# A decoder trunk on one core: due times for all work around the product stream, and attention weight tiles split in halves

## The chip, the core and the metric

The kernel runs on one core of a Trainium2 chip. The core has a matrix engine (TensorE, PE in the profile), a vector engine (VectorE, DVE), a scalar engine (ScalarE, ACT), a general engine (GpSimd, POOL) and a queue engine (SyncE, SP), each with its own instruction stream that it works off in order, and sixteen DMA engines. PE multiplies 128x128 blocks that it loads as weights (PEld) with up to 512 columns, into banks of PSUM, an accumulator memory from which DVE and ACT read. Everything else lies in SBUF. The metric is the device time of one execution in microseconds (us), lower is better.

## What is computed

A two-layer decoder trunk for 256 positions of width 2048 in float32. Layer 0 mixes by Mamba-2 SSD heads and latent attention side by side, layer 1 by stick-breaking attention; each is followed by a SwiGLU feed-forward network (FFN) of hidden width 5632. All weights are float32 and are read once.

```python
for layer in range(DEPTH):                       # DEPTH = 2
    h = rms_norm(x, mix_norm[layer])
    if layer % 2 == 0:
        mix = ssd_mla_mixer(h, w_in[e], ..., w_out_even[e], cos, sin)
    else:
        mix = stick_breaking_mixer(h, w_qkv[o], w_out_odd[o])
    x = x + mix
    f = rms_norm(x, ffn_norm[layer])
    x = x + (silu(f @ w_gate[layer]) * (f @ w_up[layer])) @ w_down[layer]
return rms_norm(x, final_norm)
```

## The kernel before

**Split products.** A float32 matrix is taken apart into a rounded part and a remainder, and each product is made of three: hi by hi, hi by lo, lo by hi. A weight tile is 4 k-tiles of 128 rows by 512 columns, 1 MB, loaded by one DMA on SP's queue. `split` (line 247) makes `wh` (a cast on ACT, line 249) and `wl` (a subtraction on DVE, line 250), each 128x2048. Activations are split in the same way after PE has transposed them (`transpose_split`, PE line 259).

**Projections.** `project` (line 333) runs over the k-tiles of a column block for two row tiles (6 matmuls of 512 columns for each k-tile, lines 340 to 342), with weights from `load_split` (line 300). After an output projection `add_residual` (line 390) adds the two accumulators to the residual `xres` (DVE line 395, one operation for each row tile), and the next layer's transposes read `xres`.

**The FFN.** `ffn` (line 550) goes over the hidden width in five blocks of 2, 2, 2, 2 and 3 column pairs; after each block come four down projections. `pair` (line 467) computes a 512-column block of gate and of up together. Over the first 8 of 16 k-tiles it uses a Strassen-like scheme of seven products, each 12 matmuls (`product`, lines 493, 494 and 498); over the last 8 the four tiles are multiplied plainly ("classical", lines 526 to 528, 24 matmuls each). The scheme needs the weight tiles b11, b22, b21 and the sums t1 = b11 + b12, t2 = t1 + b22, t3 = b12 + b22 and t4 = t2 + b21 (`wadd`, DVE line 464, 128x2048 each), all split. PE uses them in the order b11, b22, t1, b21, t2, t4, t3, then the four classical tiles. At the end of a pair `left` (h-, DVE line 558, then SiLU on ACT) and `right` (for row tile 1 H*, line 566; for row tile 0 h+, line 564, and then H*, line 566) turn the accumulators into `h`, which PE transposes in the middle of the next pair's first products.

**Where tiles lie.** A "region" of SBUF, `xp`, changes its use: in the attention layers ("acts") it holds activations, in an FFN ("sums") the sums and some weight tiles. A new region's tiles wait for the old region's last readers at the places that they overlay. `wh` and `wl` have two buffers each in the pool `weights`, and in an FFN every third tile lies in the region (`whtile`, `wltile`, lines 109 and 112). Loaded tiles `w` have three, and in an FFN one more in the region.

**What sets the order.** PE's order is that of the program text. On the other engines a scheduler orders by priority (a lower number comes first) as dependences allow. Weight work (loads, splits, sums) takes numbers from a counter, `wprio`, that starts at 100000 and rises with each piece, so it goes in the order of the text. Work marked URGENT has 50000. Everything else, the residual adds among it, has 10000000: it goes after weight work that is ready. `tick` (line 81) counts units of the product stream, `now`; background tasks (transposes, attention chains) are generators that `tick` moves on.

Of the kernel before, what the change touches and what calls it, by code (L numbers as in the profile page):

```python
# [27 lines left out]
class Trunk:  # L28
# [6 lines left out]
    def __init__(self, ctx, tc, ins, out):  # L35
        self.tc, self.nc, self.i, self.out = tc, tc.nc, ins, out
        ec = ctx.enter_context
        self.cp = ec(tc.tile_pool(name="const", bufs=1))
        self.wp = ec(tc.tile_pool(name="weights", bufs=4))
        self.ap = ec(tc.tile_pool(name="acts", bufs=42))  # L40
        self.sp = ec(tc.tile_pool(name="small", bufs=2))
        ps = bass.MemoryType.PSUM
        self.pacc = ec(tc.tile_pool(name="pacc", bufs=1, space=ps))
        self.ptr = ec(tc.tile_pool(name="ptr", bufs=4, space=ps))
        self.dp = ec(tc.tile_pool(name="scratch", bufs=1, space=bass.MemoryType.DRAM))
        self.shared, self.shared_kind = None, None
        self.region("acts")
        ctx.callback(self.region, None)
        self.banks = ["acc0", "acc1", "acc2", "acc3"]
        self.n, self.wn = 0, {}  # L50
        self.now, self.tasks = 0, []
        self.wprio = 100000
        tc.cur_priority = 10000000

    @contextmanager
    def priority(self, at):

        keep, self.tc.cur_priority = self.tc.cur_priority, at
        yield
        self.tc.cur_priority = keep  # L60


    def spawn(self, gen):
# [16 lines left out]

    def tick(self):
        self.now += 1
        ready = [t for t in self.tasks if t["wake"] <= self.now]
        for t in ready[:2]:
            if not t["done"]:
                self.advance(t)

    def region(self, kind):

        if self.shared is not None:  # L90
            self.shared.__exit__(None, None, None)
        self.shared, self.shared_kind = None, kind
        if kind:
            bufs = 20 if kind == "acts" else 2
            self.shared = self.tc.tile_pool(name=f"shared_{kind}", bufs=bufs, reuse_waits="tile")
            self.xp = self.shared.__enter__()

    def s2x(self, shape, dt=F32):

        return self.xp.tile([P, *shape], dt, name=self.nm("s2x"), tag="s2x", bufs=20)  # L100

    def wtile(self, tag="w", dt=F32, bufs=4, own=3):

        n = self.wn[tag] = self.wn.get(tag, 0) + 1
        if self.shared_kind == "sums" and n % bufs == 0:
            return self.xp.tile([P, 4, 512], dt, name=self.nm(tag), tag=tag, bufs=1)
        return self.wp.tile([P, 4, 512], dt, name=self.nm(tag), tag=tag, bufs=own)

    def whtile(self):
        return self.wtile("wh", F32R, 3, 2)  # L110

    def wltile(self):
        return self.wtile("wl", F32R, 3, 2)

    def wsum(self):
        return self.xp.tile([P, 4, 512], F32, name=self.nm("wsum"), tag="wsum", bufs=2)
# [25 lines left out]
    def constants(self):  # L142
# [4 lines left out]
        with self.priority(0):  # L147
            nc.sync.dma_start(rows_m, i["mix_norm"].rearrange("l (k p) -> (l k) p", p=P))
        for j in range(4):
            with self.priority(self.wprio + 1000 * j - 500):  # L150
                nc.sync.dma_start(self.xres[:, :, j * 512:(j + 1) * 512],
                                  i["x"][0, :, j * 512:(j + 1) * 512].rearrange("(t p) d -> p t d", p=P))
        with self.priority(self.wprio + 3500):
            self.small_loads(rows_a, rows_b)
        with self.priority(self.wprio + 6500):
# [144 lines left out]
    def load_split(self, view, nk, n):  # L300

        nc = self.nc
        for k0 in range(0, nk, 4):
            k1 = min(nk, k0 + 4)
            res = []
            with self.priority(self.wprio):
                self.wprio += 1000
                w = self.wtile()
                for dst, src in view(w, k0, k1):
                    nc.sync.dma_start(dst, src)  # L310
                order = ExitStack()
                for ins in self.first if self.wprio <= 105000 else ():
                    order.enter_context(self.tc.issue_after(ins))
                wh, wl = self.whtile(), self.wltile()
                step = 1 if self.wprio < 102000 else 2 if self.wprio < 106000 else k1 - k0
                for c in range(0, k1 - k0, step):
                    d = c + step
                    self.split(wh[:, c:d, :n], wl[:, c:d, :n], w[:, c:d, :n])
                order.close()
                for k in range(k0, k1):  # L320
                    res.append((wh[:, k - k0, :n], wl[:, k - k0, :n]))
            yield from res

    @staticmethod
# [65 lines left out]
    def add_residual(self, ps, j, scale=None):  # L390
        nc, x = self.nc, self.xres
        for t in range(2):
            xs = x[:, t, j * 512:(j + 1) * 512]
            if scale is None:
                nc.vector.tensor_tensor(xs, ps[t], xs, op=ALU.add)
            else:
                nc.vector.scalar_tensor_tensor(xs, ps[t], scale[:, t:t + 1], xs, op0=ALU.mult, op1=ALU.add)


    URGENT = 50000  # L400
# [42 lines left out]
            res.append((hi, lo))  # L443
        return res

    def wload(self, view, k0):
        w = self.wtile()
        with self.priority(self.wprio):
            self.wprio += 100
            for dst, src in view(w, k0, k0 + 4):  # L450
                self.nc.sync.dma_start(dst, src)
        return w

    def wsplit(self, w):
        wh, wl = self.whtile(), self.wltile()
        with self.priority(self.wprio):
            self.wprio += 100
            self.split(wh, wl, w)
        return wh, wl

    def wadd(self, o, p, q):
        with self.priority(self.wprio):
            self.wprio += 100
            self.nc.vector.tensor_tensor(o, p, q, op=ALU.add)
        return o

    def pair(self, st, xT, va, vb, left, right):
# [1 line left out]

        nc = self.nc  # L470
        mm = nc.tensor.matmul
        b11, b12 = self.wload(va, 0), self.wload(vb, 0)
        b22, b21 = self.wload(vb, 4), self.wload(va, 4)
        cl = [(self.wload(va, 8), self.wload(vb, 8)), (self.wload(va, 12), self.wload(vb, 12))]
        t1 = self.wadd(self.wsum(), b11, b12)
        w11 = self.wsplit(b11)
        t2 = self.wadd(self.wsum(), t1, b22)
        t3 = self.wadd(b12, b12, b22)
        w22 = self.wsplit(b22)
        wt1 = self.wsplit(t1)  # L480
# [645 lines left out]
```

## Time and profile before

| | before |
|---|---|
| device time, median of 3 runs | 2513.11 us (2512.77 to 2513.15) |
| the profiled execution's own time | 2512.09 us |
| its span in the trace | 2510.4 us |
| granted TensorE clock, mean | 0.991 |
| PE busy | 2454.1 us, 98% of the span |
| DVE busy | 1714.3 us, 68% |
| ACT busy | 1298.1 us, 52% |
| instructions | 27612 |

A row of a group or timeline has the line of the kernel, the engine, the operation, what it writes and reads, and busy time with the mean in ns, or start and duration in us. In brackets stands the idle time before an instruction and what ended it. A row of a window has the busy time and count of PE, PEld, DVE, ACT and POOL, the granted clock, the DMA share and GB/s.

### The profile page before, as it was taken

How to read it: one execution, taken by the hardware profiler on the slowest of the kernel's cores; microseconds unless marked ns; L12 is line 12 of the kernel's file. 1: busy time of each engine (PE TensorE's matmuls, PEld its weight loads, DVE VectorE, ACT ScalarE, POOL GpSimd, SP SyncE). 2: the span in 40 equal slices, each digit the busy share in tenths (PEclk: the TensorE clock that was granted, in tenths of full speed). 3: DMA queues.
4: the chain of work that ended last, by engine and by line, in shares of the span. 5: the costliest groups of instructions: out<-in, count | busy, mean ns of one | idle time of the engine just before them, and what ended most of it. 6: DMA issues, size and time to landing. Idle time of an engine off the chain costs nothing.

```text
span 2510.4 us, 27612 instructions
## 1 busy us (share of the span) xinstructions
PE 2454.1 (98%) x11176; PEld 2008.4 (80%) x11176; DVE 1714.3 (68%) x1476; ACT 1298.1 (52%) x1266; POOL 130.9 (5%) x164
## 2 busy tenths in 40 slices
PE   8999999999899999999999999999899999999998
PEld 7788877788688888888878787778688888888876
DVE  5775455456778778787965444445787878787874
ACT  6655555434554545454544545554554545454553
POOL 1231121000000000000000000000000000000001
PEclk9999999999899999999999999999999999999999
DMA  7654553355555556565554454445555656565653
GB/s 234 194 176 159 178 157 111 126 193 185 182 197 199 194 196 206 184 203 185 204 190 143 166 172 160 151 155 173 181 200 184 217 172 215 170 231 168 235 188 114
DMA packets 257824, 454.78 MB, mean 181 GB/s; under 512 B 20716, under 2 KB 45424, under 8 KB 257696
## 3 DMA queue, kind: packets, MB, share of 16 engines
q1 hardware_dynamic: 255168, 446.48, 53.1%
q0 software_dynamic: 1952, 5.48, 0.6%
q8 instruction: 88, 1.44, 0.2%
q10 hardware_dynamic: 576, 1.05, 0.1%
q14 instruction: 40, 0.33, 0.0%
HBM read 450.85 MB, written 2.13 MB: 180 GB/s over the span
## 4 chain that ended last, share of the span: by engine, by line
PE 56%; issue 39%; ACT 2%; DVE 1%; POOL 0%; DMA 0%; SPq 0%; POOLq 0%; ACTq 0%; DVEq 0%
PE acc L341 11%; PE acc L340 11%; PE acc L342 11%; PE acc L527 3%; PE acc L526 3%; PE acc L528 3%; PE acc L493 3%; PE acc L494 3%; PE acc L498 3%; PE tr L259 1%; ACT wh L249 1%; DVE wl L250 1%; PE at L1049 1%; PE at L978 1%; PE at L1048 0%
## 5 line engine op out<-in xcount | busy, mean ns | idle before, releaser
L250 DVE TENSOR_TENSOR wl<-w,wh 128x2048 fp32r<-128x2048 f32 (+2 forms) x431 | 966.3, 2250 | 578.3 <-ACT wh L249 569.5
L249 ACT CAST wh<-w 128x2048 fp32r<-128x2048 f32 (+2 forms) x431 | 807.3, 1875 | 732.5 <-PE acc L342 414.8
L340 PE MATMUL acc<-wh,s 128*128 128x512 f32 (+1 forms) x1728 | 692.2, 401 | 3.3 <-ACT wh L249 3.3
L341 PE MATMUL acc<-wl,s 128*128 128x512 f32 (+1 forms) x1728 | 673.6, 390 | 7.0 <-DVE wl L250 6.9
L342 PE MATMUL acc<-wh,s 128*128 128x512 f32 (+1 forms) x1728 | 674.2, 390 | 0.0
L341 PEld LDWEIGHTS acc<-wl,s 128*128 128x128 f32 x1728 | 326.2, 189 | 74.4 <-DVE wl L250 10.3
L342 PEld LDWEIGHTS acc<-wh,s 128*128 128x128 f32 x1728 | 325.3, 188 | 70.2
L340 PEld LDWEIGHTS acc<-wh,s 128*128 128x128 f32 x1728 | 325.9, 189 | 67.6 <-ACT wh L249 4.1
L528 PE MATMUL acc<-wl,s 128*128 128x512 f32 x704 | 275.3, 391 | 0.0
L527 PE MATMUL acc<-wh,s 128*128 128x512 f32 x704 | 275.2, 391 | 0.0
L526 PE MATMUL acc<-wh,s 128*128 128x512 f32 x704 | 275.2, 391 | 0.0
L493 PE MATMUL acc<-wh,s 128*128 128x512 f32 x616 | 246.4, 400 | 0.0
L494 PE MATMUL acc<-wh,s 128*128 128x512 f32 x616 | 242.4, 393 | 0.0
L249 ACT CAST wh<-wsum 128x2048 fp32r<-128x2048 f32 x66 | 125.9, 1910 | 84.6 <-PE acc L527 35.7
L498 PE MATMUL acc<-wl,s 128*128 128x512 f32 x616 | 166.1, 391 | 0.0
L250 DVE TENSOR_TENSOR wl<-wsum,wh 128x2048 fp32r<-128x2048 f32 x66 | 150.6, 2285 | 13.8 <-ACT wh L249 13.8
L527 PEld LDWEIGHTS acc<-wh,s 128*128 128x128 f32 x704 | 132.2, 188 | 29.1
L526 PEld LDWEIGHTS acc<-wh,s 128*128 128x128 f32 x704 | 132.2, 188 | 29.0
L528 PEld LDWEIGHTS acc<-wl,s 128*128 128x128 f32 x704 | 132.1, 188 | 29.0
L493 PEld LDWEIGHTS acc<-wh,s 128*128 128x128 f32 x616 | 116.9, 190 | 25.6
L494 PEld LDWEIGHTS acc<-wh,s 128*128 128x128 f32 x616 | 117.0, 190 | 24.3
L498 PEld LDWEIGHTS acc<-wl,s 128*128 128x128 f32 x616 | 115.8, 188 | 25.7
(246 smaller groups left out, 2063.3 us busy)
## 6 DMA issues: line engine op xcount, KB each, us to landing
w<-in_w_gate_dram SPq DMA_DIRECT2D x88, 1024.0 KB, 5.1
w<-in_w_up_dram SPq DMA_DIRECT2D x88, 1024.0 KB, 5.1
w<-in_w_down_dram SPq DMA_DIRECT2D x88, 1024.0 KB, 5.0
w<-in_w_qkv_dram SPq DMA_DIRECT2D x48, 1024.0 KB, 5.0
w<-in_w_in_dram SPq DMA_DIRECT2D x47, 1024.0 KB, 5.2
w<-in_w_out_even_dram SPq DMA_DIRECT2D x32, 1024.0 KB, 4.9
w<-in_w_out_odd_dram SPq DMA_DIRECT2D x16, 1024.0 KB, 5.0
w<-in_w_ukv_dram SPq DMA_DIRECT2D x32, 256.0 KB, 4.1
```

The lines of the kernel that those rows point to most:

```text
L249: nc.scalar.copy(hi, src)
L250: nc.vector.tensor_tensor(lo, src, hi.bitcast(F32), op=ALU.subtract)
L259: self.nc.tensor.transpose(pt[:, k, t * P:(t + 1) * P], src(t, 2 * k2 + k), self.ident)
L340: nc.tensor.matmul(ps[t], hi[:, ts], wh, start=k == 0, stop=False)
L341: nc.tensor.matmul(ps[t], hi[:, ts], wl, start=False, stop=False)
L342: nc.tensor.matmul(ps[t], lo[:, ts], wh, start=False, stop=k == nk - 1)
L493: mm(ps, hi[:, k], wh[:, k], start=start and k == 0, stop=False, skip_group_check=True)
L494: mm(ps, lo[:, k], wh[:, k], start=False, stop=False, skip_group_check=True)
L498: mm(ps, hi[:, k], wl[:, k], start=False, stop=k == 3, skip_group_check=True)
L526: mm(ps, hi, wh, start=False, stop=False, skip_group_check=True)
L527: mm(ps, lo, wh, start=False, stop=False, skip_group_check=True)
L528: mm(ps, hi, wl, start=False, stop=stop, skip_group_check=True)
```

## The change

The counter goes. A piece of weight work is now due at a unit of the product stream: `due(units)` is 100000 + 250 x (now + units). `tick` sets the number of all other work to `due(4)`, so it stands among the weight work instead of behind all of it. The residual adds become URGENT. `wh` and `wl` move into the region altogether (`part`): in attention layers as halves of 2 k-tiles with 4 buffers each, in an FFN as whole tiles with 3 buffers each, all in the region. `load_split` splits a tile in two halves in attention layers. `pair` loads b11, b22, b12, b21 in this order, and splits and sums are written in the order in which PE needs them, with due offsets. Nothing on PE changes. The instructions that the halves add are 155 on ACT and 155 on DVE.

```diff
-        self.n, self.wn = 0, {}
+        self.n = self.wn = 0
-        self.wprio = 100000
+        self.base = 100000
         tc.cur_priority = 10000000
+    def due(self, units):
+        return self.base + 250 * (self.now + units)
     def priority(self, at):
...
     def tick(self):
         self.now += 1
+        self.tc.cur_priority = self.due(self.SLACK)
         ready = [t for t in self.tasks if t["wake"] <= self.now]
         for t in ready[:2]:
             if not t["done"]:
...
     def region(self, kind):
         if self.shared is not None:
             self.shared.__exit__(None, None, None)
         self.shared, self.shared_kind = None, kind
         if kind:
-            bufs = 20 if kind == "acts" else 2
-            self.shared = self.tc.tile_pool(name=f"shared_{kind}", bufs=bufs, reuse_waits="tile")
+            self.shared = self.tc.tile_pool(name=f"shared_{kind}", bufs=2, reuse_waits="tile")
             self.xp = self.shared.__enter__()
     def s2x(self, shape, dt=F32):
         return self.xp.tile([P, *shape], dt, name=self.nm("s2x"), tag="s2x", bufs=20)
-    def wtile(self, tag="w", dt=F32, bufs=4, own=3):
-        n = self.wn[tag] = self.wn.get(tag, 0) + 1
-        if self.shared_kind == "sums" and n % bufs == 0:
-            return self.xp.tile([P, 4, 512], dt, name=self.nm(tag), tag=tag, bufs=1)
-        return self.wp.tile([P, 4, 512], dt, name=self.nm(tag), tag=tag, bufs=own)
-    def whtile(self):
-        return self.wtile("wh", F32R, 3, 2)
-    def wltile(self):
-        return self.wtile("wl", F32R, 3, 2)
+    def wtile(self):
+        self.wn += 1
+        pool, bufs = (self.xp, 1) if self.shared_kind == "sums" and self.wn % 4 == 0 else (self.wp, 3)
+        return pool.tile([P, 4, 512], F32, name=self.nm("w"), tag="w", bufs=bufs)
+    def part(self, tag):
+        nk, bufs = (2, 4) if self.shared_kind == "acts" else (4, 3)
+        return self.xp.tile([P, nk, 512], F32R, name=self.nm(tag), tag=tag, bufs=bufs)
     def wsum(self):
         return self.xp.tile([P, 4, 512], F32, name=self.nm("wsum"), tag="wsum", bufs=2)
...
         for k0 in range(0, nk, 4):
             k1 = min(nk, k0 + 4)
             res = []
-            with self.priority(self.wprio):
-                self.wprio += 1000
+            with self.priority(self.due(0)):
                 w = self.wtile()
                 for dst, src in view(w, k0, k1):
                     nc.sync.dma_start(dst, src)
                 order = ExitStack()
-                for ins in self.first if self.wprio <= 105000 else ():
+                for ins in self.first if self.now < 16 else ():
                     order.enter_context(self.tc.issue_after(ins))
-                wh, wl = self.whtile(), self.wltile()
-                step = 1 if self.wprio < 102000 else 2 if self.wprio < 106000 else k1 - k0
-                for c in range(0, k1 - k0, step):
-                    d = c + step
-                    self.split(wh[:, c:d, :n], wl[:, c:d, :n], w[:, c:d, :n])
+                np = 2 if self.shared_kind == "acts" else 4
+                for a in range(k0, k1, np):
+                    b = min(k1, a + np)
+                    wh, wl = self.part("wh"), self.part("wl")
+                    step = 1 if self.now < 4 else np
+                    for c in range(0, b - a, step):
+                        d = min(c + step, b - a)
+                        self.split(wh[:, c:d, :n], wl[:, c:d, :n], w[:, a - k0 + c:a - k0 + d, :n])
+                    for k in range(a, b):
+                        res.append((wh[:, k - a, :n], wl[:, k - a, :n]))
                 order.close()
-                for k in range(k0, k1):
-                    res.append((wh[:, k - k0, :n], wl[:, k - k0, :n]))
             yield from res
     @staticmethod
...
         nc, x = self.nc, self.xres
         for t in range(2):
             xs = x[:, t, j * 512:(j + 1) * 512]
-            if scale is None:
-                nc.vector.tensor_tensor(xs, ps[t], xs, op=ALU.add)
-            else:
-                nc.vector.scalar_tensor_tensor(xs, ps[t], scale[:, t:t + 1], xs, op0=ALU.mult, op1=ALU.add)
+            with self.priority(self.URGENT):
+                if scale is None:
+                    nc.vector.tensor_tensor(xs, ps[t], xs, op=ALU.add)
+                else:
+                    nc.vector.scalar_tensor_tensor(xs, ps[t], scale[:, t:t + 1], xs, op0=ALU.mult, op1=ALU.add)
     URGENT = 50000
...
             res.append((hi, lo))
         return res
-    def wload(self, view, k0):
+    def wload(self, view, k0, at):
         w = self.wtile()
-        with self.priority(self.wprio):
-            self.wprio += 100
+        with self.priority(self.due(at)):
             for dst, src in view(w, k0, k0 + 4):
                 self.nc.sync.dma_start(dst, src)
         return w
-    def wsplit(self, w):
-        wh, wl = self.whtile(), self.wltile()
-        with self.priority(self.wprio):
-            self.wprio += 100
+    def wsplit(self, w, at):
+        wh, wl = self.part("wh"), self.part("wl")
+        with self.priority(self.due(at)):
             self.split(wh, wl, w)
         return wh, wl
-    def wadd(self, o, p, q):
-        with self.priority(self.wprio):
-            self.wprio += 100
+    def wadd(self, o, p, q, at):
+        with self.priority(self.due(at)):
             self.nc.vector.tensor_tensor(o, p, q, op=ALU.add)
         return o
...
         nc = self.nc
         mm = nc.tensor.matmul
-        b11, b12 = self.wload(va, 0), self.wload(vb, 0)
-        b22, b21 = self.wload(vb, 4), self.wload(va, 4)
-        cl = [(self.wload(va, 8), self.wload(vb, 8)), (self.wload(va, 12), self.wload(vb, 12))]
-        t1 = self.wadd(self.wsum(), b11, b12)
-        w11 = self.wsplit(b11)
-        t2 = self.wadd(self.wsum(), t1, b22)
-        t3 = self.wadd(b12, b12, b22)
-        w22 = self.wsplit(b22)
-        wt1 = self.wsplit(t1)
-        t4 = self.wadd(self.wsum(), t2, b21)
-        w21 = self.wsplit(b21)
-        wt2, wt4, wt3 = self.wsplit(t2), self.wsplit(t4), self.wsplit(t3)
+        b11, b22, b12, b21 = (self.wload(*a) for a in ((va, 0, 0), (vb, 4, 2), (vb, 0, 4), (va, 4, 6)))
+        cl = [(self.wload(va, 8, 14), self.wload(vb, 8, 18)), (self.wload(va, 12, 22), self.wload(vb, 12, 26))]
+        w11, w22 = self.wsplit(b11, 0), self.wsplit(b22, 2)
+        t1 = self.wadd(self.wsum(), b11, b12, 4)
+        wt1 = self.wsplit(t1, 4)
+        w21 = self.wsplit(b21, 6)
+        t2 = self.wadd(self.wsum(), t1, b22, 8)
+        wt2 = self.wsplit(t2, 8)
+        wt4 = self.wsplit(self.wadd(self.wsum(), t2, b21, 10), 10)
+        wt3 = self.wsplit(self.wadd(b12, b12, b22, 12), 12)
         self.join(st["xT"][0][0])
         self.join(st["xT"][1][0])
         z, p3, p2, p4 = self.banks
...
         for half in range(2):
             k0, last = 8 + 4 * half, half == 1
             for side in range(2):
-                wh, wl = self.wsplit(cl[half][side])
+                wh, wl = self.wsplit(cl[half][side], 0)
                 if not last:
                     for k in range(4):
                         for t, ps in enumerate((p2, p4) if side == 0 else (p3, z)):
```

The instructions move in these places, all on DVE. In the rows `wl` is a split's remainder, `wsum` or a `w` written from two tiles a sum of weights, `xres` a residual add, and `s` from `acc` a step of `h`.

The start of the first FFN, around the end of the attention layer's last output projection (the two `xres` rows). Before:

```order
L250 TENSOR_TENSOR wl_5152<-w_5133,wh_5151 128x2048
L395 TENSOR_TENSOR xres<-acc_4941,xres 128x512
L464 TENSOR_TENSOR wsum_5149<-w_5133,w_5135 128x2048
L250 TENSOR_TENSOR wl_5159<-w_5137,wh_5158 128x2048
L464 TENSOR_TENSOR wsum_5155<-wsum_5149,w_5137 128x2048
L464 TENSOR_TENSOR w_5135<-w_5135,w_5137 128x2048
L250 TENSOR_TENSOR wl_5163<-wsum_5149,wh_5162 128x2048
L395 TENSOR_TENSOR xres<-acc_4942,xres 128x512
```

Now:

```order
L255 TENSOR_TENSOR wl_5436<-w_5429,wh_5435 128x1024
L403 TENSOR_TENSOR xres<-acc_5299,xres 128x512
L403 TENSOR_TENSOR xres<-acc_5300,xres 128x512
L469 TENSOR_TENSOR wsum_5531<-w_5507,w_5511 128x2048
L255 TENSOR_TENSOR wl_5524<-w_5507,wh_5523 128x2048
L255 TENSOR_TENSOR wl_5528<-w_5509,wh_5527 128x2048
L255 TENSOR_TENSOR wl_5534<-wsum_5531,wh_5533 128x2048
```

Both residual adds moved ahead of the first pair's work; the split of b11, which stood ahead of them (`wl_5152`), moved behind them.

The change from the first to the second pair of the second block. Before, from the sum t2 on:

```order
L464 TENSOR_TENSOR wsum_7079<-wsum_7073,w_7061 128x2048
L558 TENSOR_TENSOR s_1193_6856<-acc_6842,s_1193_6856 128x512
L250 TENSOR_TENSOR wl_7076<-w_7057,wh_7075 128x2048
L558 TENSOR_TENSOR s_1196_6935<-acc_6843,s_1196_6935 128x512
L464 TENSOR_TENSOR w_7059<-w_7059,w_7061 128x2048
L566 SCALAR_TENSOR_TENSOR s_1196_6935<-acc_6840,rstd_5125,s_1196_6935 128x512
L250 TENSOR_TENSOR wl_7083<-w_7061,wh_7082 128x2048
L564 TENSOR_TENSOR s_1195_6909<-acc_6841,s_1195_6909 128x512
L566 SCALAR_TENSOR_TENSOR s_1193_6856<-s_1195_6909,rstd_5125,s_1193_6856 128x512
```

Now:

```order
L255 TENSOR_TENSOR wl_6620<-w_6603,wh_6619 128x2048
L561 TENSOR_TENSOR s_1259_6402<-acc_6388,s_1259_6402 128x512
L561 TENSOR_TENSOR s_1262_6481<-acc_6389,s_1262_6481 128x512
L469 TENSOR_TENSOR wsum_6637<-wsum_6627,w_6605 128x2048
L569 SCALAR_TENSOR_TENSOR s_1262_6481<-acc_6386,rstd_5499,s_1262_6481 128x512
L255 TENSOR_TENSOR wl_6624<-w_6605,wh_6623 128x2048
L567 TENSOR_TENSOR s_1261_6455<-acc_6387,s_1261_6455 128x512
L469 TENSOR_TENSOR w_6607<-w_6607,w_6605 128x2048
L569 SCALAR_TENSOR_TENSOR s_1259_6402<-s_1261_6455,rstd_5499,s_1259_6402 128x512
```

The sums t2 and t3 each come one step of `h` later; t3 (`w_6607`) now stands between h+ (L567) and the last H* (L569). The sum t4 moved as well, from ahead of the split of b21 to behind that of t2.

The end of the first layer's FFN and the start of the stick-breaking layer. Before:

```order
L250 TENSOR_TENSOR wl_9729<-w_9726,wh_9728 128x2048
L270 SCALAR_TENSOR_TENSOR s_1614_9664<-tr_9658,vm,s_1613_9663 128x256 x2
L270 SCALAR_TENSOR_TENSOR s_1617_9681<-tr_9675,vm,s_1616_9680 128x256 x2
L250 TENSOR_TENSOR wl_9767<-w_9764,wh_9766 128x2048
L250 TENSOR_TENSOR wl_9823<-w_9820,wh_9822 128x2048
L395 TENSOR_TENSOR xres<-acc_9638,xres 128x512
L395 TENSOR_TENSOR xres<-acc_9639,xres 128x512
```

Now:

```order
L255 TENSOR_TENSOR wl_10103<-w_10100,wh_10102 128x2048
L275 SCALAR_TENSOR_TENSOR s_1806_10038<-tr_10032,vm,s_1805_10037 128x256 x2
L275 SCALAR_TENSOR_TENSOR s_1809_10055<-tr_10049,vm,s_1808_10054 128x256 x2
L403 TENSOR_TENSOR xres<-acc_10012,xres 128x512
L403 TENSOR_TENSOR xres<-acc_10013,xres 128x512
L255 TENSOR_TENSOR wl_10141<-w_10138,wh_10140 128x1024
L255 TENSOR_TENSOR wl_10145<-w_10138,wh_10144 128x1024
```

The attention layer's first two splits (`wl_9767`, `wl_9823`) stood ahead of the last residual adds; the first half (`wl_10141`) now stands behind them.

More of the change, by code (lines that the diff above doesn't have):

```diff
@@ L60, in priority @@
         self.tc.cur_priority = keep
+    SLACK = 4
     def spawn(self, gen):
@@ L149, in constants @@
         for j in range(4):
-            with self.priority(self.wprio + 1000 * j - 500):
+            with self.priority(self.base + 1000 * j - 500):
                 nc.sync.dma_start(self.xres[:, :, j * 512:(j + 1) * 512],
                                   i["x"][0, :, j * 512:(j + 1) * 512].rearrange("(t p) d -> p t d", p=P))
-        with self.priority(self.wprio + 3500):
+        with self.priority(self.base + 3500):
             self.small_loads(rows_a, rows_b)
-        with self.priority(self.wprio + 6500):
+        with self.priority(self.base + 6500):
             self.wdt = []
```

## The prediction, made before the changed kernel ran

> **What bounds the kernel now.** I read the page first (busy shares), then the waits of PE, then windows of 40 us, then the timelines of DVE, ACT and PE around each gap.
>
> ```profile
> PE 2454.1 (98%) x11176; PEld 2008.4 (80%) x11176; DVE 1714.3 (68%) x1476; ACT 1298.1 (52%) x1266; POOL 130.9 (5%) x164
> PE tr L259 <- DVE xres L395: 22.7, 2, 11.4
> PE acc L341 <- DVE wl L250: 8.7, 6, 1.8
> PE acc L340 <- ACT wh L249: 4.3, 5, 1.1
> PE tr L259 <- DVE s L566: 4.3, 2, 2.2
> 600.00:640.00 40.00, 40.00 (x178) 32.48 (x177) 26.40 (x25) 19.91 (x22) 0.00 (x0) 1.00 0.56 187
> 640.00:680.00 40.00, 28.65 (x120) 23.20 (x119) 33.90 (x28) 23.37 (x23) 0.00 (x0) 0.83 0.50 174
> 1240.00:1280.00 40.00, 37.81 (x163) 30.67 (x162) 35.81 (x23) 23.57 (x18) 0.00 (x0) 0.96 0.54 182
> 1760.00:1800.00 40.00, 28.54 (x123) 23.02 (x122) 27.99 (x26) 19.25 (x25) 0.00 (x0) 0.87 0.46 157
> 2360.00:2400.00 40.00, 37.89 (x170) 30.93 (x169) 36.45 (x24) 22.28 (x17) 0.00 (x0) 1.00 0.59 207
> L250 DVE TENSOR_TENSOR wl<-w,wh 128x2048 fp32r<-128x2048 f32 x415 | 949.3, 2295 | 573.1 <-ACT wh L249 564.3 <-DMA w<-in_w_ukv_dram 5.1 <-PE acc L528 3.4
> L249 ACT CAST wh<-w 128x2048 fp32r<-128x2048 f32 x415 | 792.7, 1910 | 725.0 <-PE acc L342 409.9 <-PE acc L527 119.3 <-DVE xres L395 66.0
> ```
>
> PE is the bound: 2454.1 us busy. An undisturbed window holds 178 matmuls in 40 us, about 0.227 us each with the odd record missing, so a Strassen product of 12 takes 2.73. The change keeps PE's order and work, so all it can move is the idle time: two waits of 11.4 us at the FFN starts (22.7), two of 2.2 at pair changes (4.3), and 13.0 on `wl` and `wh`, mostly in the stick-breaking layer. Not all of that can be had: the rest of PE's idle time is the start and the end.
>
> **FFN starts (gain).** DVE, then PE:
>
> ```profile
> 640.43 0.69 DVE L395 TENSOR_TENSOR xres<-acc,xres 128x512 f32<-128x512 f32 x1 [0.65 <-PE acc L342]
> 641.04 2.28 DVE L464 TENSOR_TENSOR wsum<-w,w 128x2048 f32<-128x2048 f32 x1
> 649.85 2.28 DVE L250 TENSOR_TENSOR wl<-wsum,wh 128x2048 fp32r<-128x2048 f32 x1
> 652.05 0.68 DVE L395 TENSOR_TENSOR xres<-acc,xres 128x512 f32<-128x512 f32 x1
> 640.71 0.40 PE L342 MATMUL acc<-wh,s2x 128*128 128x512 f32 x1
> 652.79 1.76 PE L259 MATMUL tr<-ident,xres 128*128 128x128 f32 x7 [11.28 <-DVE xres L395]
> 675.00 0.39 PE L526 MATMUL acc<-wh,s 128*128 128x512 f32 x1
> ```
>
> The second residual add stands behind five operations of 2.28 us that start every 2.20 (641.04 to 652.05). From the projection's end E (640.71 + 0.23 = 640.94) to the first classical tile at 675.00 there are 34.1 us; unstalled it would be eight transposes (1.76) and 7 x 2.73 = 20.9. The loss is 13.2; the second FFN start, whose window is alike, gives 12.5 by the same walk. After the change both residual adds come first, so the transposes end at E+2.65. But no split and no sum of the first pair is ahead of the residuals any more (the `wh`, `wl` and `wsum` tiles now lie in the region that the projection still uses). DVE pays them in line: `wsum` to E+3.05, `wl11` 5.2, `wl22` 7.4, `wl` of t1 9.6; ACT casts 1.91 each and copies z between them. My walk has the third product over at 13.9, the splits of t2, t4, t3 at 20.8, 25.5, 27.9, and the classical tile effectively at E+29.9: a loss of 9.0. Gain 4.2 + 3.5 = 7.7. Bounds: all 25.7 (the first pair is split early after all) to a loss of 3 (one more 2.28 in line at some point).
>
> **Pair changes (loss).** In each FFN block the next pair begins on PE while DVE finishes `h` of the last: h+ (L564), then H* (L566), then PE's transposes. C is the end of the pair's last matmul. First a change without a stall (953.21 is C - 0.39), then the one with:
>
> ```profile
> 951.86 2.28 DVE L250 TENSOR_TENSOR wl<-w,wh 128x2048 fp32r<-128x2048 f32 x1
> 954.06 0.68 DVE L564 TENSOR_TENSOR s<-acc,s 128x512 f32<-128x512 f32 x1
> 954.77 0.75 DVE L566 SCALAR_TENSOR_TENSOR s<-s,rstd,s 128x512 f32<-128x512 f32 x1
> 953.21 0.39 PE L528 MATMUL acc<-wl,s 128*128 128x512 f32 x1
> 956.23 0.60 PE L259 MATMUL tr<-ident,s 128*128 128x128 f32 x4
> 1252.80 0.68 DVE L564 TENSOR_TENSOR s<-acc,s 128x512 f32<-128x512 f32 x1
> 1254.14 2.29 DVE L250 TENSOR_TENSOR wl<-wsum,wh 128x2048 fp32r<-128x2048 f32 x1 [0.66 <-ACT wh L249]
> 1256.35 0.74 DVE L566 SCALAR_TENSOR_TENSOR s<-s,rstd,s 128x512 f32<-128x512 f32 x1
> 1251.94 0.39 PE L528 MATMUL acc<-wl,s 128*128 128x512 f32 x1
> 1257.24 0.63 PE L259 MATMUL tr<-ident,s 128*128 128x128 f32 x4 [2.19 <-DVE s L566]
> 1257.62 0.48 PE L493 MATMUL acc<-wh,s 128*128 128x512 f32 x1
> ```
>
> With h+ and H* side by side H* ends at C+1.92 and the transposes, due at C+2.63, wait for nothing: 0.7 us of slack. At 1252 one split stands between them, and PE waits 2.19. In the order of before that is so at two of the twelve changes, the two with the 4.3 us of waits. In the new order each of the twelve has an operation of 2.28 us there: in blocks 2 to 4, and the first change of block 5, the sum t3; in block 1 and the second change of block 5 a split of t1. So h+ runs C+0.46 to 1.14, the sum holds DVE until C+3.3, H* ends at C+4.05 and the transposes start at 4.2, a stall of 1.6. Nothing can hide that: h+ needs the accumulator that C closes, DVE runs in order, and PE has one product (2.73 us) to do meanwhile. The split type stalls 2.35 as measured (start to start).
>
> Behind it DVE is a big operation later than before, and the sum t4 now stands after `wl` of t2: 14.5 us after C, its cast (1.91) ends at 16.5, `wl` of t4 at 18.7, where PE, 1.6 late, wants the cast at 15.9. The last classical split ends at 23.1 against 22.8 wanted. That is 1.4 to 1.6 more: about 3.2 per change. Block 1, by the same walk from 2.35, comes to 3.9. The second change of block 5 had 2.35 already, and gains 1.5 in cost. Per FFN 3.9 + 4 x 3.2 + 1.5 = 18.2, for two 36.4. Lower bound, the first stall alone: 2 x (2.35 + 4 x 1.6) = 17.5. Upper bound: two operations of 2.28 late at each of the ten new places, 2 x 5 x 4.6 = 46, and 1.5 more at the two old ones, 49. I take 36.4, as both parts follow from an order that is fixed. After the stall at 1257 the matmuls start 0.32 to 0.43 apart for some 3 us, and the window's granted clock is 0.96; the other stall (2360 to 2400) left it at 1.00. I take 0.3 a change, +3.5 in all; bounds 0 and 12 x 1.8 = 21.6.
>
> The Trainium skill ("TensorE: Matmul & The Clock Gate", Part 1) says that the array falls to half rate after an idle window of about 3.4 us and is back after as long a busy one. By that rule the new stalls, all under 3.4, would cost no clock, and the sum would be 3.5 lower; the trace agrees at 2392 and not at 1257.
>
> **Stick-breaking layer (gain).**
>
> ```profile
> 1440.00:1480.00 40.00, 37.65 (x171) 31.28 (x172) 21.04 (x20) 19.91 (x23) 0.00 (x0) 0.96 0.48 158
> L250 DVE TENSOR_TENSOR wl<-w,wh 128x1024 fp32r<-128x1024 f32 x12 | 14.4, 1220 | 5.3 <-ACT wh L249 5.2
> L249 ACT CAST wh<-w 128x1024 fp32r<-128x1024 f32 x12 | 12.3, 1051 | 7.5 <-PE acc L342 5.0 <-DMA w<-in_w_ukv_dram 1.5 <-DMA w<-in_w_in_dram 0.8
> 1513.60 0.53 ACT L691 ACTIVATE s<-s 128x384 f32<-128x384 f32 x1 [2.24 <-POOL s L689]
> 1518.48 1.90 ACT L249 CAST wh<-w 128x2048 fp32r<-128x2048 f32 x1
> 1520.43 0.49 PE L340 MATMUL acc<-wh,s 128*128 128x512 f32 x1 [1.01 <-ACT wh L249]
> 1522.76 0.50 PE L341 MATMUL acc<-wl,s 128*128 128x512 f32 x1 [1.83 <-DVE wl L250]
> ```
>
> At each of four V projections the cast stands behind the chain of POOL's selects and ACT's exponentials; PE waits 1.01 and 1.83, 3.3 start to start. A half takes 1.05 and 1.22 instead of 1.91 and 2.295, 0.9 and 1.1 less, but the chain stays ahead of the cast and the second half's cast follows it: about 1.9 of the 3.3 stay, gain 4 x 1.4 = 5.6, bounds 0 and 13. In the even layer, whose waits are the rest of the 13.0 and gaps of 0.4 us, halves take about 3.5; bounds -1 and 6. At the second layer's start the two residual adds (which wait for the projection's end) now stand ahead of the first attention split: 0.69 + 0.6 and half a split on DVE put `wl` 2.0 us behind that end, and PE 1.8; bounds 0 and 4. The 155 extra instructions on ACT and DVE are these halves: 155 x (2 x 1.22 - 2.295) = 22 us more on DVE and 30 on ACT. The window shows both half idle beside PE there (21.04 and 19.91 of 40), so I cost them at nothing; without that cover they would be those 22 to 30.
>
> **Sum:** 36.4 + 3.5 - 7.7 - 5.6 - 3.5 + 1.8 = +24.9 on the profiled 2512.1: 2537.0. The runs' median (2513.1) lies 1.0 above the profiled execution, so 2538.
>
> **Rivals.** *The later part of each pair change is hidden* (0.19): only the first stall counts, because t4's cast and split finish in time. For it: the chain is late by only 0.3 to 1 us at each step; against: t4's sum, cast and split follow one another, 2.2 + 1.9 + 2.2, with nothing to overlap them. With clock 2 and 15.0 of gains: 2513 + 17.5 + 2 - 15 = about 2518, or 2513 to 2523. *The gains win* (0.24; not slower): the first pair of each FFN is ready at E+2.7, because the casts there start as soon as the projection's next-to-last matmul is done and residuals no longer wait. FFN starts give 24, stick-breaking 11, the even layer 5, against 17.5: 2490 to 2507. It decides if the splits of t1 and t2 keep up with PE, that is if DVE needs under 2.73 per product; five splits and sums for the first three products speak against it. *The new order does nothing on balance* (0.07), gains and stalls half as large as I have them: 2508 to 2518. *Cold after every stall* (0.07): 1.8 us at all twelve instead of the mean of 0.3: 2538 + 12 x 1.5 = 2556.
>
> **How the numbers follow.** My forecast, 2538, has 0.43; its own range is 2525 to 2551. Two runs of this kernel can be told apart from 0.2% on, 5 us. Faster 0.24; within 0.2% the 0.07 and 0.05 of the first rival, 0.12; slower the rest, 0.64. The range reaches down into the faster case and up to the forecast's dearer end: 2499 to 2553.
>
> **What would show it.** Waits of PE: the transposes on DVE's H* twelve times at 1.6 to 2.4 us instead of two; no 11-us wait on the residual, but waits on `wl` and `wh` in the first pair after it; DVE's timeline with a 2.28-us operation between h+ and H*; halves as 128x1024 groups. Wrong if those transposes start without a wait, or if the first pair's splits run before the residuals.

## The result and the profile after

| | before | after |
|---|---|---|
| device time, median | 2513.13 us (2512.77 to 2519.43, 4 runs) | 2549.49 us (2547.41 to 2552.76, 4 runs) |
| ratio | 1 | 1.014, 95% interval 1.0121 to 1.0159 |
| the profiled execution's span | 2510.4 us | 2547.3 us |
| granted TensorE clock, mean | 0.991 | 0.996 |
| PE busy | 2454.1 us | 2492.2 us |

The change made the kernel 36 us slower; the forecast was 25 slower. Most of it does not come from where the forecast had it. First the changed kernel's page (busy time) and its waits of PE (us in total, times, longest):

```profile
PE 2492.2 (98%) x11176; PEld 2002.5 (79%) x11176; DVE 1737.2 (68%) x1631; ACT 1318.9 (52%) x1421; POOL 129.3 (5%) x164
PE tr L264 <- DVE s L569: 17.7, 12, 2.2
PE acc L501 <- DVE wl L255: 8.7, 18, 1.6
PE acc L496 <- ACT wh L254: 5.4, 10, 1.8
PE acc L348 <- DVE wl L255: 2.1, 2, 1.7
PE tr L264 <- DVE xres L403: 0.7, 2, 0.4
PE acc L347 <- ACT wh L254: 0.6, 1, 0.6
```

The waits changed much as forecast: twelve on H* (L569) instead of two, the two of 11.4 us on the residual down to 0.4 each, new ones on splits inside the Strassen products (L496, L501), and the 13.0 us on `wh` and `wl` of the projections down to 2.7. But in sum the waits that PE names are about as long as before (45 us against 47). What grew by 38 us is PE's **busy** time, with the same 11176 instructions and a higher granted clock. One group shows it: a third of the classical matmuls, first of the kernel before, then of the changed one.

```profile
L527 PE MATMUL acc<-wh,s 128*128 128x512 f32 x704 | 275.2, 391 | 0.0
```

```profile
L529 PE MATMUL acc<-wh,s 128*128 128x512 f32 x704 | 277.9, 395 | 0.0
```

The mean of one went from 391 to 395 ns. PE is pipelined, so what counts is the time from one start to the next: over the 512-column matmuls on split tiles whose successor starts within 0.3 us, its mean is 229.2 ns before and 232.5 after. The program has 9816 matmuls on split tiles, of which some 9300 have such a successor: 9816 x 3.3 ns is about 33 us of the 36.9 between the spans. The rest, some 4 us, is what losses and gains of the order leave on balance.

**FFN start**, changed kernel; PE, then DVE:

```profile
642.64 0.39 PE L349 MATMUL acc<-wh,s2x 128*128 128x512 f32 x1
643.81 0.98 PE L264 MATMUL tr<-ident,xres 128*128 128x128 f32 x7 [0.35 <-DVE xres L403]
672.09 0.40 PE L529 MATMUL acc<-wh,s 128*128 128x512 f32 x1
642.39 1.37 DVE L403 TENSOR_TENSOR xres<-acc,xres 128x512 f32<-128x512 f32 x2 [7.89 <-PE acc L349]
643.67 2.28 DVE L469 TENSOR_TENSOR wsum<-w,w 128x2048 f32<-128x2048 f32 x1
645.87 4.48 DVE L255 TENSOR_TENSOR wl<-w,wh 128x2048 fp32r<-128x2048 f32 x2
```

Both residual adds run at once and the transposes follow, but DVE idles 7.89 us ahead of them, and the first pair's sum and splits come after. From the projection's last matmul to the first classical one there are 29.45 us instead of 34.29 (second FFN 29.45 instead of 33.66).

**Pair change**, changed kernel; DVE, then PE:

```profile
963.95 0.68 DVE L567 TENSOR_TENSOR s<-acc,s 128x512 f32<-128x512 f32 x1
964.55 2.28 DVE L469 TENSOR_TENSOR w<-w,w 128x2048 f32<-128x2048 f32 x1
966.75 0.74 DVE L569 SCALAR_TENSOR_TENSOR s<-s,rstd,s 128x512 f32<-128x512 f32 x1
963.31 0.39 PE L531 MATMUL acc<-wl,s 128*128 128x512 f32 x1
963.54 0.40 PE L496 MATMUL acc<-wh,s 128*128 128x512 f32 x1
967.63 0.63 PE L264 MATMUL tr<-ident,s 128*128 128x128 f32 x4 [1.13 <-DVE s L569]
```

The sum t3 stands between h+ (L567) and H* (L569), and PE waits 1.13 us. The two starts 963.31 and 963.54 are 0.23 apart in both kernels to two digits; the 5 ns do not show in a timeline row, only in a mean.

**Stick-breaking layer.** PE's sum over four windows of 80 us (1400 to 1720), before and then changed:

```profile
sum 320.00, PE 308.85 PEld 255.13 DVE 151.91 ACT 165.99 POOL 18.91; mean PE 77.21 PEld 63.78 DVE 37.98 ACT 41.50 POOL 4.73
```

```profile
sum 320.00, PE 320.00 PEld 263.80 DVE 164.69 ACT 181.88 POOL 9.68; mean PE 80.00 PEld 65.95 DVE 41.17 ACT 45.47 POOL 2.42
```

The 11.15 us of idle PE are gone altogether.

### The profile page after: what moved, and what is told of

Read it like the earlier page. It is cut to its first block, busy times and chain, and to the rows that moved or that the text cites. A ratio compares the mean times of both kernels' runs of the same rounds, so it can differ in the third digit from the quotient of the medians.

```text
span 2547.3 us, 28045 instructions
## 1 busy us (share of the span) xinstructions
PE 2492.2 (98%) x11176; PEld 2002.5 (79%) x11176; DVE 1737.2 (68%) x1631; ACT 1318.9 (52%) x1421; POOL 129.3 (5%) x164
## 4 chain that ended last, share of the span: by engine, by line
PE 84%; DVE 9%; ACT 3%; issue 2%; DMA 1%; POOL 0%; SPq 0%; ACTq 0%; DVEq 0%; POOLq 0%
PE acc L347 18%; PE acc L349 18%; PE acc L348 18%; PE acc L531 5%; PE acc L530 5%; PE acc L529 5%; DVE wl L255 5%; PE acc L501 3%; PE acc L496 3%; PE acc L497 3%; ACT wh L254 2%; DVE wsum L469 1%; PE tr L264 1%; DVE w L469 1%; PE at L1052 1%
## 5 line engine op out<-in xcount | busy, mean ns | idle before, releaser
L255 DVE TENSOR_TENSOR wl<-w,wh 128x1024 fp32r<-128x1024 f32 (+2 forms) x586 | 999.9, 1712 | 582.3 <-ACT wh L254 580.9
L254 ACT CAST wh<-w 128x1024 fp32r<-128x1024 f32 (+2 forms) x586 | 831.6, 1425 | 836.0 <-PE acc L349 469.8
L348 PE MATMUL acc<-wl,s 128*128 128x512 f32 (+1 forms) x1728 | 679.0, 393 | 2.2 <-DVE wl L255 2.1
L348 PEld LDWEIGHTS acc<-wl,s 128*128 128x128 f32 x1728 | 325.7, 189 | 73.5 <-DVE wl L255 3.6
L531 PE MATMUL acc<-wl,s 128*128 128x512 f32 x704 | 279.4, 397 | 2.6 <-DVE wl L255 2.1
L530 PE MATMUL acc<-wh,s 128*128 128x512 f32 x704 | 278.0, 395 | 0.0
L529 PE MATMUL acc<-wh,s 128*128 128x512 f32 x704 | 277.9, 395 | 0.0
L496 PE MATMUL acc<-wh,s 128*128 128x512 f32 x616 | 250.0, 406 | 7.3 <-ACT wh L254 5.4
L497 PE MATMUL acc<-wh,s 128*128 128x512 f32 x616 | 244.5, 397 | 0.0
L501 PE MATMUL acc<-wl,s 128*128 128x512 f32 x616 | 172.0, 401 | 8.7 <-DVE wl L255 8.7
L501 PEld LDWEIGHTS acc<-wl,s 128*128 128x128 f32 x616 | 115.9, 190 | 43.6 <-DVE wl L255 16.9
L496 PEld LDWEIGHTS acc<-wh,s 128*128 128x128 f32 x616 | 116.8, 190 | 41.2 <-ACT wh L254 11.2
L497 PEld LDWEIGHTS acc<-wh,s 128*128 128x128 f32 x616 | 116.9, 190 | 24.9
```

The source lines that it names most:

```text
L254: nc.scalar.copy(hi, src)
L255: nc.vector.tensor_tensor(lo, src, hi.bitcast(F32), op=ALU.subtract)
L348: nc.tensor.matmul(ps[t], hi[:, ts], wl, start=False, stop=False)
L496: mm(ps, hi[:, k], wh[:, k], start=start and k == 0, stop=False, skip_group_check=True)
L497: mm(ps, lo[:, k], wh[:, k], start=False, stop=False, skip_group_check=True)
L501: mm(ps, hi[:, k], wl[:, k], start=False, stop=k == 3, skip_group_check=True)
```

## Why a matmul takes longer: four kernels with padding

The matmuls sort by one property. (Counts of matmuls here and below hold to a few, their means to 0.1 ns.) Each reads a moving tile (`wh` or `wl`, 512 columns of 4 bytes) and loads a stationary tile (activations). In the kernel before, `wh` and `wl` lie mostly in the pool `weights`, in the changed one all in the region. Their start addresses in a partition, as the built programs have them, differ by whole multiples of 512 bytes for 6581 of the matmuls before (mean 227.7 ns) and by 128 or 384 for 2737 (232.5 to 232.8). After, by a multiple of 512 for 734 (227.4 ns) and by 128 for 8516 (233.0). **Theory A** is that this difference sets the pace; the rivals are the place in SBUF or the waits for it (B), and stalls (C). Unused bytes between two pools move one pool against the other and leave every instruction where it is:

```diff
 # after_p384, before_p384: 96 floats; after_p128: 32 floats, ahead of the region
+        self.sp.tile([P, 96], F32, name="pad", tag="pad", bufs=1)
 # before_a128: 32 floats, ahead of the activations, behind the weights
+        self.ap.tile([P, 32], F32, name="pad", tag="pad", bufs=1)
```

> 384 unused bytes per partition between the pool of activations and the region; no instruction changes its place. Theory A (a 512-column matmul costs about 5 ns more when the start addresses of its moving tile, wh or wl, and its stationary tile differ by something other than a multiple of 512 bytes; here all 9815 of them then differ by a multiple): the mean pitch in the feed-forward layers falls from 233 to 228 ns, and the time by about 8516 x 5.3 = 45 us, from 2549 to 2502 to 2508 us. Rival B (tiles in the region are slow because the region lies high in SBUF, or because its buffers are waited for): the region only moves up by 384 bytes, so the time stays at 2545 to 2553. Rival C (the added time is stalls by the new order): the same, 2545 to 2553.

> The kernel before with the same 384 bytes. Theory A: its 2011 matmuls at 128 and 725 at 384 bytes of difference lose about 5 ns each, 14 us: 2497 to 2502 us. Rivals B and C: 2511 to 2515.

> The kernel before with 128 unused bytes ahead of the activations, so that the weight tiles and the activations, which differed by a multiple of 512 for 7007 matmuls, now differ by 384 more; the order stays. Theory A: 6581 measured matmuls cost 5.3 ns more, +35 us, 2543 to 2552; 768 matmuls come to a difference of 256 and tell that one. Rivals B and C: 2511 to 2515.

> The changed kernel with 128 bytes of padding: 9047 matmuls have a difference of 256 instead of 128. Theory A with a period of 512 bytes: still 232 to 233 ns, 2543 to 2553 us. Theory A with a period of 256 bytes: 227 to 228 ns, 2502 to 2508 us. Rivals B and C: 2545 to 2553.

| kernel | us, median | ratio to before, 95% | matmuls and mean ns from start to start, by the difference modulo 512 |
|---|---|---|---|
| before_p384 | 2499.06 | 0.9942 (0.9926 to 0.9959) | 0: 9305 at 227.3 |
| before_a128 | 2545.90 | 1.0136 (1.0119 to 1.0153) | 128: 2015 at 233.2; 256: 732 at 227.0; 384: 6570 at 232.9 |
| after_p384 | 2526.27 | 1.0054 (1.0039 to 1.0069) | 0: 9231 at 227.5 |
| after_p128 | 2520.99 | 1.0033 (1.0020 to 1.0045) | 0: 734 at 227.2; 256: 8497 at 227.5 |

The same kind of group row in three of them, before_p384, before_a128 and after_p384 in this order:

```profile
L527 PE MATMUL acc<-wh,s 128*128 128x512 f32 x704 | 273.9, 389 | 0.0
```

```profile
L527 PE MATMUL acc<-wh,s 128*128 128x512 f32 x704 | 278.0, 395 | 0.0
```

```profile
L529 PE MATMUL acc<-wh,s 128*128 128x512 f32 x704 | 274.0, 389 | 0.0
```

Theory A stands and B falls: 128 bytes make the kernel before 33 us slower, 384 bytes in another place make it 14 faster, with the same order of instructions. The 391 ns of the kernel before are a mixture: two thirds of the FFN's tiles at 389 (own buffers), one third at 394 (region). A difference of 256 is as good as none, so the period is 256 bytes. The changed kernel, though, came to 2526 (after_p384) and 2521 (after_p128) and not to 2502 to 2508: its matmuls are at 227.5 ns, but its waits on H* grew from 17.7 us to this (after_p384):

```profile
PE tr L264 <- DVE s L569: 27.6, 12, 3.4
```

The twelve pair changes take 14 us more than in the changed kernel; 10 of it are these waits, and behind several of them matmuls stand 0.43 us apart. A faster PE gives DVE less time, and the new order's stalls, partly covered by the slow matmuls, come out: over the 180 matmuls of a pair, 5.5 ns are 1 us, and the wait of the eight common changes grew on average by that (1.1 to 2.2 us). This is worked out, not tested by itself. At equal pace the order costs 2526.27 - 2499.06 = 27 us, or 22 by after_p128, whose eight runs reach from 2514 to 2527.

**How fine the difference is.** Two more kernels have 8 and 16 floats in the place of before_a128's 32.

> The kernel before with 32 unused bytes ahead of the activations: 7007 matmuls then have weight tile and activation 224 bytes apart by a period of 256 (the region's stay at 128). If any difference costs 5 ns: +33 to 37 us, 2544 to 2550, as with 128 bytes. If only bit 7 of the two start addresses has to agree (they end in hexadecimal 40 and 60 here): 227 ns as before, 2511 to 2516 us. If the cost grows with the difference: between, 2518 to 2535.

> The same with 64 bytes: 192 apart by a period of 256, and the starts end in hexadecimal 40 and 80. Any difference, or bit 7: 2544 to 2550 us. If the cost grows with the difference: between that of 32 and of 128 bytes.

They took 2549.76 us (ratio 1.0145, 1.0131 to 1.0159) and 2544.82 (1.0126, 1.0113 to 1.0140). The 6575 matmuls 224 apart (modulo 256) have 233.2 ns, the 6573 at 192 the same; 725 at 96 have 233.4, 732 at 64 have 229.2. So neither one address bit nor the size of the difference alone decides; the differences of 96, 128, 192 and 224 all cost 5 to 6 ns. Only the 64 is milder, and only one group of matmuls in one kernel had it.

## Which part of the order costs, and which gains

All five kernels here have the 384 bytes, so that pace plays no part.

**The pair changes.** after_p384_h puts three things on DVE behind the last H* of the pair before:

```diff
+    def behind(self):
+        return ExitStack() if self.lasth is None else self.tc.issue_after(self.lasth.ins)
...
-        wt1 = self.wsplit(t1, 4)
+        with self.behind():
+            wt1 = self.wsplit(t1, 4)
...
-        wt3 = self.wsplit(self.wadd(b12, b12, b22, 12), 12)
+        with self.behind():
+            wt3 = self.wsplit(self.wadd(b12, b12, b22, 12), 12)
...
-            nc.vector.scalar_tensor_tensor(h[t], c, rstd[:, t:t + 1], h[t], op0=ALU.mult, op1=ALU.mult)
+            self.lasth = nc.vector.scalar_tensor_tensor(h[t], c, rstd[:, t:t + 1], h[t], op0=ALU.mult, op1=ALU.mult)
```

> The changed kernel with the padding of 384 bytes, and with the split of t1, the sum t3 and its split issued on DVE behind the last H* of the pair before, so that h+ and H* stand side by side at every pair change. Theory O (at PE's full pace the new order's cost of 27 us, 2526 against 2499, is mostly the pair changes): the waits of the transposes on H*, 27.6 us in 12 times, go to under 3 in all, and the time falls by 20 to 27, to 2499 to 2506 us. Rival D (DVE is short of time in the feed-forward layers, whatever stands where): what no longer waits at the transposes waits a little later for wl, and the time falls by under 8 us, 2518 to 2526.

2504.01 us, ratio to before 0.9967 (0.9954 to 0.9980): 22 off, inside theory O's band. Its waits:

```profile
PE acc L503 <- ACT s L514: 14.8, 10, 1.6
PE acc L508 <- DVE wl L255: 8.7, 17, 1.6
PE acc L503 <- ACT wh L254: 7.3, 13, 1.9
PE tr L264 <- DVE s L576: 3.7, 8, 0.8
```

The waits on H* fell from 27.6 to 3.7, so rival D fails as the main cause. But a new wait of 14.8 us on the copy of the accumulator z (L514) has come, ten times 1.5. ACT, then PE, at one change:

```profile
954.24 1.90 ACT L254 CAST wh<-wsum 128x2048 fp32r<-128x2048 f32 x1 [1.25 <-issue]
956.05 0.57 ACT L514 COPY s<-acc 128x512 f32<-128x512 f32 x1
956.68 0.50 PE L503 MATMUL acc<-wh,s 128*128 128x512 f32 x1 [1.59 <-ACT s L514]
```

By the built program's order the cast is that of t2, and the copy is queued behind it; in after_p384 the copy stands ahead of it (960.11 and 963.36). So holding back work on DVE moved the scheduler's order on ACT as well. The sum t2 had been ready since 946.8. The `wh` of t2 has the address that b22's had, and PE starts the last matmul that reads b22's at 953.77: the cast most likely waited for that buffer, though the profile does not name it. The forecast has no term for this wait.

**Halves alone.** before_p384_halves keeps tiles, buffers and priorities of before and only splits in two steps:

```diff
-                step = 1 if self.wprio < 102000 else 2 if self.wprio < 106000 else k1 - k0
+                step = 1 if self.wprio < 102000 else 2 if self.wprio < 106000 or self.shared_kind == "acts" else k1 - k0
```

> The padded kernel before with its attention layers' splits done in two steps of 2 k-tiles, in the same tiles and by the same priorities. If the halves alone are what took the waits of the V projections away (13 us in the trace of the changed kernel): 12 to 14 us off, 2485 to 2488. If it was the buffers (four halves) or the due times: under 5 us off, 2494 to 2499.

2478.68 us, ratio 0.9870 (0.9856 to 0.9885): 20 us off, more than expected. PE's sum over the same four windows:

```profile
sum 320.00, PE 320.00 PEld 266.64 DVE 169.03 ACT 181.48 POOL 12.29; mean PE 80.00 PEld 66.66 DVE 42.26 ACT 45.37 POOL 3.07
```

The halves are what took the waits of the V projections away; neither four buffers nor due times are needed for it. The 20 us are more than the 13 of named waits because most of these stalls also slow what follows: from ahead of the stall over the next 24 matmuls before_p384 takes 9.85, 11.49, 10.19 and 8.72 us, with matmuls 0.43 apart for a while after three of the four; with halves it takes 5.33 to 5.50, which is 18.6 us less in all. The first of the four in before_p384:

```profile
1431.19 0.50 PE L340 MATMUL acc<-wh,s 128*128 128x512 f32 x1 [0.65 <-ACT wh L249]
1433.52 0.50 PE L341 MATMUL acc<-wl,s 128*128 128x512 f32 x1 [1.82 <-DVE wl L250]
1435.97 0.63 PE L342 MATMUL acc<-wh,s 128*128 128x512 f32 x1
1436.40 0.63 PE L340 MATMUL acc<-wh,s 128*128 128x512 f32 x1
```

**Urgent residual adds alone.** before_p384_res gives the two adds the number 50000 and changes nothing else.

> The padded kernel before with the residual adds at the URGENT number, nothing else; wh and wl stay in their own buffers. In its order the first FFN has both residual adds behind the first split of the pair and ahead of the rest. If the new FFN starts lose what they still lose (9 and 8 us) because no tile of the first pair can be split before the projection ends: here the first split is done by then, each start loses 4 to 6 instead of 13, and the time falls by 13 to 18 us, 2481 to 2486. If it is the sums in line after the residuals: about the gain of the changed kernel, 9 to 11 us, 2488 to 2490.

2496.00 us, ratio 0.9940 (0.9924 to 0.9957), 3 us off: neither expectation held. The 22.6 us of waits on the residual are gone and this has come in their place:

```profile
PE acc L494 <- ACT s L505: 18.6, 6, 4.6
```

The third product needs the bank that ACT copies (L505), and ACT has casts of sums and the last block's transposes and squares queued ahead of that copy. The first split being ready early was worth next to nothing: from the projection's last matmul to the first classical one the two starts take 33.0 us each instead of 34.1 and 34.3.

**Together.** best1 has halves, urgent adds and the split of t1 behind H*; best2 is best1 without the urgent adds.

> The padded kernel before with halves, urgent residual adds, and the split of t1 behind the last H* of the pair before. If the three gains add up (12, 15, and 4 to 6 from two pair changes): 2466 to 2470 us. If DVE then binds in the feed-forward layers: 2475 to 2485.

> The padded kernel before with the halves (2478.7 us) and with the split of t1 behind the last H* of the pair before, which puts h+ and H* side by side at all twelve pair changes; the residual adds as before. If the waits of the transposes on H*, 5.8 us in that kernel's trace, come from the two changes where the split of t1 stood between them: 2472 to 2476 us. If they only move to wl or wh a little later: 2477 to 2480.

best1 took 2478.51 us, ratio 0.9865 (0.9851 to 0.9880), no better than halves alone: its waits on the copy of z are 19.4 us. best2 took 2473.68 us (2473.33 to 2478.45, 5 runs), ratio 0.9843 (0.9830 to 0.9857). It beats both kernels of this study, by 1.6% and 3.0%. Its gain over halves alone, 5 us, is at the edge of what the runs tell apart, and its profiled execution (2476.5 us of span, the slowest of the five) does not bear out the cause expected: 6.8 us of waits on H* were still seen there. So the halves and the padding carry it. What would still be to be had:

```profile
PE tr L259 <- DVE xres L395: 22.6, 2, 11.4
```

A start of the FFN that moves the residual adds, the copies of z and the casts on ACT together was not tried.

## Why the prediction was right, and where it was not

The direction and the range hold, and the size roughly, but not for the reason forecast: the largest term was missing, and one premise is wrong.

- **"The change keeps PE's order and work, so all it can move is the idle time" failed.** Moving `wh` and `wl` to the region changed what one matmul costs: 33 of the 36.9 us. I had noted the move and read it only for what can be split early. The trace of before held the evidence: matmuls on tiles in the region take 233 ns and those on tiles outside 227, in both FFNs. Even the window that I read as undisturbed (600 to 640) is a slow one: of its 178 matmuls 8 are short transposes, and the 170 long ones stand 0.232 us apart. The 0.227 holds for FFN tiles outside the region.
- **Pair changes:** 36.4 forecast. From the end of a pair to the next first classical tile, the twelve changes take 251.5 us before and 283.0 after; 4.4 of the 31.5 are pace, so 27 are stalls. With both kernels at 227 ns it is 251.0 against 297.4, 46 us. The mechanism is the one forecast (a sum between h+ and H*, then t4 late), and the forecast size lies between the two. The eight changes of the common kind lose 2.2 us each in the changed kernel, not 3.2 (about 1.2 for H* and 1.0 for t4), and 2.9 to 5.5 at the faster pace.
- **FFN starts:** 7.7 of gain forecast, 9.0 measured (4.8 and 4.2). That the first pair's splits would be done in line after the residuals is what the timeline shows.
- **Stick-breaking layer:** 5.6 of gain forecast with a bound of 13. Measured 17: the four stretches of 24 matmuls take 38.8 us before and 21.5 after. The term was mis-sized twice. The waits vanish altogether, and most of them brought matmuls at about half pace behind them that I had left out of the sum here, though I priced them elsewhere.
- **Second layer's start:** 1.8 of loss forecast; the one wait of 1.7 on `wl` (L348) is it. **Even layer:** 3.5 of gain forecast, 3.8 measured from start to start over the first 400 us.
- **Clock after new stalls:** 3.5 forecast. At three of the four changes with a stall of 2.1 to 2.2 us matmuls stand 0.43 us apart behind it, and these changes take 24.9 to 25.0 us where the fourth takes 23.3. The kernel before had one such change, so some 3 us are new (an estimate from these times). None of the eight stalls of 1.1 had this, so the rival "cold after every stall" is out. The mean granted clock rose all the same, to 0.996, since the two long stalls and the V projections' went.
- **Rivals:** "the gains win" failed at the place named, since five sums and splits for the first products do not keep up with PE. "The later part is hidden" is partly seen: t4 costs about 1.0 us a change instead of 1.4 to 1.6.

The order's terms as measured come to about nothing in the changed kernel (27 - 9 - 17 - 4 + 2 = -1; the spans leave some 4), where the forecast had 25, and the 33 us come from a cost that it put at nothing. That 25 lay near 36, and that the time fell into the range, is luck. At equal pace, where the order costs 22 to 27, the sum's total fits, though not its terms.

Counted from before_p384 (2499 us), the order by itself costs 27 (after_p384), the slow pace by itself 47 (before_a128), and both together 50 (the changed kernel). They overlap, most likely because PE's slower pace gives DVE the time that the order takes from it.

## What to carry to other kernels

When PE is the bound and its order is unchanged, first compare the mean time of one matmul in the same group of both kernels: a few ns times ten thousand can outweigh all that an order gains or loses. When a tile moves to another pool, look at its start address against that of the operand it is multiplied with, not only at when its buffer is free. And weigh a stall with the pace after it: a wait of 3 us here cost up to 6.

## What the runs showed of the hardware

A matmul of 512 columns of 4 bytes (float32r in the program), streamed behind the load of its 128x128 stationary tile, takes 227 to 228 ns from start to start when the start addresses of its moving and of the stationary tile agree modulo 256 bytes, and 232 to 233.4 when they differ by 96, 128, 192 or 224 (229.2 at 64). This held in eight kernels, in two pools and in both directions: tiles in the region against activations in the region ran at 227.4, tiles in the region against activations in another pool at 233.0. Why it is so, and whether the load that follows or the one before counts, was not separated.

Stalls differ in what follows them. Three windows of the changed kernel, the first with the stall of 2.1 us of a split between h+ and H*, the second with one of 1.1 us, the third with another of 2.1 us (the last three columns are granted clock, DMA share and GB/s):

```profile
680.00:720.00 40.00, 37.69 (x159) 29.72 (x157) 33.18 (x21) 20.97 (x17) 0.00 (x0) 0.96 0.40 135
800.00:840.00 40.00, 38.86 (x172) 31.14 (x171) 34.14 (x23) 22.46 (x17) 0.00 (x0) 1.00 0.60 202
1840.00:1880.00 40.00, 37.16 (x162) 29.12 (x161) 33.18 (x20) 22.00 (x17) 0.00 (x0) 1.00 0.55 193
```

After the eight stalls of 1.1 us the clock stayed at 1.00. After three of the four of 2.1 to 2.2, and after the 3.3 (two waits, from start to start) of the V projections in some groups and not in others, it fell, and 4 to 11 matmuls stood 0.43 us apart. The Trainium skill ("TensorE: Matmul & The Clock Gate", Part 1) says that activity is watched in windows of about 3.4 us that run on their own and do not start with the kernel's work. That equal stalls slow what follows at one time and not at another agrees with it. That 2.1 us can be enough does not agree with the whole idle window of about 3.4 us that its Part 1 names for the fall.
